# A hybrid attention and RWKV block on one core: the row factor on VectorE, low-rank weights split ahead, the second key norm inside the first half's recursion

## The chip, the cores and the metric

The kernel runs on one core of a Trainium2 chip. Its engines work side by side, each through its own queue of instructions in order: TensorE (PE) multiplies matrices into PSUM, VectorE (DVE), ScalarE (ACT) and GpSimd (POOL) work elementwise, and SyncE (SP) issues most of the transfers. The metric is device time in microseconds (us) of one execution; the time of a kernel is the median of several runs.

## What is computed

One layer over 256 tokens with a width of 2048, in fp32. Cut to what matters here:

```python
u = rms_norm(x)
proj = u @ w_in          # q, k, v of two attentions; r, k, v and low-rank inputs of RWKV-7; 3 branch gates
y_a = stick_breaking_attention(q_a, k_a, v_a)      # 4 heads of 128
y_b = forgetting_attention(q_b, k_b, v_b, log_f)   # 4 heads of 128

# RWKV-7: 16 heads of 64, chunks of 64 tokens
z = z + (z_prev - z) * mu
w_log = -softplus(-(w0 + tanh(wd) @ w_up)) - 0.5
a = sigmoid(a0 + ad @ a_up)
g = sigmoid(gd) @ g_up
kk = k * k_k
k = k * (1 + (a - 1) * k_a)
kk = kk / maximum(sqrt(sum(kk * kk)), 1e-12)       # the key norm, per head
state = state * w_t - (state @ kk_t) kka_t^T + v_t k_t^T;  y_t = state @ r_t
y_c = (group_norm(y) * ln_w + ln_b + bonus) * g    # the gate norm

m = g_a * (y_a @ w_a) + g_b * (y_b @ w_b) + g_c * (y_c @ w_c)
x = x + rms_norm(m @ w_out)
x = x + rms_norm(relu(rms_norm(x) @ w_up)**2 @ w_down)
```

## The kernel before

**Weights.** All weights are fp32 and stream from memory in halves of 128 x 1024 (512 KB), loaded on SP's queue (L145, three buffers `raw`). Each half is split into a high part `whi` on ACT (L152) and a low part `wlo` on DVE (L153), three buffers each; `wnext` keeps one half split ahead. A unit (`unit`, L178) multiplies two halves by the 16 packed parts `upk` of the normalized input: L168 for the high parts, L172 for the low ones, L176 for the last. Projections whose result is wanted with tokens on the partitions, and the branches, go through `tok` (L214, L198).

**The row factor.** The input is not normalized before the projections. The factor of each row, `rstd`, is made by `norm` (L375) from squares that `squares` sums on ACT and DVE, and is multiplied in behind each projection by `scaled` (L394), on POOL. The first eight units are the stick-breaking queries and keys (loop at L404), their output combined by `evac`. The projections of RWKV go through `shift` (L580): L585 on ACT, L586 on DVE, `scaled` at L587, L588 on ACT, L589 on DVE.

**What sets the order.** The order of PE's instructions is that of the code (L250). That of the other engines is set by a list scheduler. Beside the stream of weights run threads, Python generators: `tick` (L125) moves a clock by the estimated time of each pair of matmuls, and a thread goes on when its pause, the number that it last yielded, is over, or, where it yielded a name, some time after `mark` has set that name. The thread `mixers` (L959) runs the two attentions, the low-rank inputs (`rwkv_lora`, L596) and the RWKV in two halves of four head pairs each (`rwkv_half`, L627). `start` begins another thread; `finish` (L131) lets the clock run until no thread is left, here at L1062, before the third branch.

**A half of RWKV.** `rwkv_half` begins with the key norm: squares of the four keys (L655), split (L660, L661), summed per head by matmuls with `bones` (L668), then Ln and Exp on ACT (L672, L675) with a load of ACT's function table each (ACT_TABLE_LOAD), and a Newton step on DVE (L680 to L685). Then, for each pair, the low-rank up-projection L696 with the split weights `wl`; they are part of the tile `lows`. `lora_load` (L635) loads them on ACT's DMA queue and `lora_split` (L642) splits them: L645 on ACT, L647 twice on DVE. For the first pair the split stands behind the key norm (L689), for the others inside the pair before (L736). After the pairs comes a recursion of 31 steps on DVE (L792), then the loop over four chunks (L843): each chunk runs L847, the copies `rhs` (L851, L852), L860, the copies into `XT` (L864 on ACT, L865 on DVE, two of each), and L872, L876 and L881, which read `XT`. Behind the last chunk the thread `gate_norm` (L897) is started; the second half's key norm runs at the same time as the first half's gate norm. The second half waits for that before its chunks (L765).

**Around it.** Stick-breaking attention's sums are masked on POOL (L448, eight pieces), then split: L454 on ACT (`sbh`), L455 on DVE. The third branch (L1064 on) needs all of the gate norms' outputs `yc`.

Of the kernel before, what the change touches and what calls it, by code (L numbers as in the profile page):

```python
# [10 lines left out]
F32 = mybir.dt.float32  # L11
F32R = mybir.dt.float32r
# [38 lines left out]
def hybrid_block(ctx, tc, xt, x, gains, params, consts, lora, gup, wst, out):  # L51
# [13 lines left out]
    def nm(s):  # L65
        uid[0] += 1
        return f"{s}_{uid[0]}"
# [4 lines left out]
    def mps():  # L72
        return pm.tile([128, 512], F32, tag="mps", name=nm("mps"), bufs=4)
# [17 lines left out]
    def P(name, i=0, r=slice(0, 128)):  # L91
        return par[r, PC[name] + i:PC[name] + i + 1]
# [6 lines left out]
    def mark(key, value=True):  # L99
        done[key], at[key] = value, clock[0]  # L100
# [121 lines left out]
    def pin(ins):  # L222
        return tc.keep_in_program_order(ins)
# [168 lines left out]
        V.tensor_scalar(rt[:, :, 1], rt[:, :, 0], 0.5, None, ALU.mult)  # L392

    def scaled(d):  # L394
        G.tensor_tensor(d, d, rstd[0:d.shape[0]], ALU.mult)

    for i in range(2):
        wsplit(wraw())
# [5 lines left out]
    for h in range(8):  # L404
        ps = qb[h] if h < 3 else unit(upk)
        qk.append(g1())
        evac(ps, qk[h])
        if h == 3:
            ms = norm()
        if h == 5:  # L410
            turned_rstd(ms)
        for i in range(h + 1) if h == 3 else [h] if h > 3 else []:
            scaled(qk[i])
    done["sbq"], done["sbk"] = qk[:4], qk[4:]

# [208 lines left out]
        done["low"] = ((lows[:, 0], lows[:, 2]), (lows[:, 1], xal), lows[:, 3].rearrange("p (a b) -> p a b", a=2))  # L624
        yield 2.0

    def rwkv_half(hf):  # L627
        PR = range(4 * hf, 4 * hf + 4)
        xw, xa, wl = done["low"]
        kn, kx = {}, {}  # L630
        B6 = rp.tile([128, 6, T], F32, tag="b6", name=nm("b6"), bufs=1)
        rin = [B6[:, i, :] for i in range(4)]
        lor = {}

        def lora_load(p):  # L635
            if p in PR:
                lor[p] = rp.tile([128, 2, 128], F32, tag="zx", name=nm("lor"), bufs=1)
                for r in (0, 64):
                    nc.scalar.dma_start(out=lor[p][r:r + 64], in_=lora.rearrange("(s r) c -> r s c", s=2)
                                        [:, :, p * 128:p * 128 + 128])  # L640

        def lora_split(p):  # L642
            if p in PR:
                raw = lor[p]
                pin(A.activation(wl, raw, AF.Copy))  # L645
                for i, r in enumerate((slice(64, 128), slice(0, 64))):
                    V.tensor_tensor(wl[r, i], raw[r, i], wl[r, i].bitcast(F32), ALU.subtract)  # L647

        lora_load(PR[0])
        if hf:  # L650
            yield 8.0
        for i, p in enumerate(PR):
            yield f"k{p}"
            kx[p] = done[f"k{p}"]
            A.activation(rin[i], kx[p], AF.Square, scale=P("kk", p))  # L655
        sq, sqh = [], []
        for i2 in range(2):
            s = B6[:, 2 * i2:2 * i2 + 2, :]
            hl = [rp.tile([128, 2, T], F32R, tag="BK", name=nm("sqh"), bufs=8) for _ in range(2)]
            A.activation(hl[0], s, AF.Copy)  # L660
            V.tensor_tensor(hl[1], s, hl[0].bitcast(F32), ALU.subtract)  # L661
            sqh.append(hl)
        yield 3.8
        for i2 in range(2):
            ri = B6[:, 2 * i2:2 * i2 + 2, :]
            ps = mps()
            for n, part in enumerate(sqh[i2]):
                PE.matmul(ps.rearrange("p (a b) -> p a b", a=2), bones, part, start=n == 0, stop=n == 1)  # L668
            sq.append(rp.tile([128, 2, T], F32, tag="At", name=nm("sq"), bufs=2))
            V.tensor_scalar(sq[i2], ps.rearrange("p (a b) -> p a b", a=2), 1e-24, None, ALU.max)  # L670
# [7 lines left out]
        for i2 in range(2):  # L678
            ri = B6[:, 2 * i2:2 * i2 + 2, :]
            V.tensor_scalar(ri, ri, 1024.0, None, ALU.mult)  # L680
            V.tensor_tensor(sc, ri, ri, ALU.mult)
            yield 2.0
            V.tensor_tensor(sc, sc, sq[i2], ALU.mult)
            V.tensor_scalar(sc, sc, -0.5, 1.5, ALU.mult, ALU.add)
            V.tensor_tensor(ri, ri, sc, ALU.mult)  # L685
            yield 3.0
        SC = rp.tile([128, 32, 128], F32, tag="SC", name=nm("SC"), bufs=1)
# [155 lines left out]
        for c in range(4):  # L843
            if c:
                for i, p in enumerate(PR):
                    for h, hc in enumerate(HC):
                        PE.matmul(xy[h][HC[i % 2 ^ h], 64 * (i // 2):64 * (i // 2) + 64], Bt[p][hc, c, 0:64],  # L847
                                  PB[hc, i, hc], start=False, stop=i >= 2)
            rhs = rp.tile([64, 2, 2, 2, 64], F32, tag="rh", name=nm("rh"), bufs=1)
            for g, hg in enumerate(HC):  # L850
                A.activation(rhs[:, 0, g], xy[0][hg, 0:128].rearrange("p (a b) -> p a b", a=2), AF.Copy)  # L851
                V.tensor_copy(rhs[:, 1, g], xy[1][hg, 0:128].rearrange("p (a b) -> p a b", a=2))  # L852
            yield 2.0
            more = known(c + 1) if c < 3 else iter([None] * 9)
            if c < 3:
                first = next(more)
            ps = mps()
            for i in range(4):
                for h, hc in enumerate(HC):
                    PE.matmul(ps[hc, 64 * i:64 * i + 64], SC[0:64, i * 8 + h * 4 + c, 0:64],  # L860
                              rhs[:, h, i % 2 ^ h, i // 2], start=i == 0, stop=i == 3)
                    xy = next(more)
            for d in range(2):
                A.activation(XT[d][0:64, :, c, HC[0]], duo(ps, HC[0], d), AF.Copy)  # L864
                V.tensor_copy(XT[d][0:64, :, c, HC[1]], duo(ps, HC[1], d))  # L865
            yield 2.2
            ps = mps()
            psp, psy = ps[:, 0:256], ps[:, 256:512]
            if c < 3:
                for i, p in enumerate(PR):  # L870
                    for h, hc in enumerate(HC):
                        PE.matmul(psp[hc, 64 * i:64 * i + 64], Kt[p][:, c, hc], XT[i // 2][:, i % 2, c, hc],  # L872
                                  start=i == 0, stop=i == 3)
            for i, p in enumerate(PR):
                for h, hc in enumerate(HC):
                    PE.matmul(psy[hc, 64 * i:64 * i + 64], XT[i // 2][:, i % 2, c, hc], SC[:, i * 8 + h * 4 + c, 64:128],  # L876
                              start=i == 0, stop=c == 0 and i == 3)
            if c:
                for i, p in enumerate(PR):
                    for h, hc in enumerate(HC):  # L880
                        PE.matmul(psy[hc, 64 * i:64 * i + 64], PB[:, i, hc], Bt[p][:, c, 64:128], start=False,  # L881
                                  stop=i == 3)
            if c < 3:
                for h, hc in enumerate(HC):
                    s, e = PB[hc, :, hc], ecol[hc, :, c:c + 1].to_broadcast([64, 4, 64])
# [770 lines left out]
```

## Time and profile before

| | |
|---|---|
| median of 3 runs | 1519.44 us (1519.37 to 1525.15) |
| the profiled execution | 1523.08 us |
| its span, first to last instruction | 1521.3 us |
| mean granted TensorE clock | 0.990 |
| ACT, share of the span | 62% |
| L153, the low parts, on DVE | 501 of 1232 ns |
| L152, the high parts, on ACT | 501 of 1056 ns |
| weight halves through SP's queue | 499, 4.3 us from issue to landing |

A row of the timeline gives start, duration, engine, line, operation, the tile written, the tile read, shapes and count, and in brackets the idle time before it with what ended it. Names in it are those of tiles, without numbers. Consecutive instructions of one kind are one row. Durations overlap a little, since an instruction's end is drained while the next begins. The granted clock is TensorE's, as a share of full speed.

### The profile page before, as it was taken

How to read it: one execution, taken by the hardware profiler on the slowest of the kernel's cores; microseconds unless marked ns; L12 is line 12 of the kernel's file. 1: busy time of each engine (PE TensorE's matmuls, PEld its weight loads, DVE VectorE, ACT ScalarE, POOL GpSimd, SP SyncE). 2: the span in 40 equal slices, each digit the busy share in tenths (PEclk: the TensorE clock that was granted, in tenths of full speed). 3: DMA queues.
4: the chain of work that ended last, by engine and by line, in shares of the span. 5: the costliest groups of instructions: out<-in, count | busy, mean ns of one | idle time of the engine just before them, and what ended most of it. 6: DMA issues, size and time to landing. Idle time of an engine off the chain costs nothing.

```text
span 1521.3 us, 22774 instructions
## 1 busy us (share of the span) xinstructions
PE 1489.9 (98%) x8401; PEld 1253.3 (82%) x8401; DVE 1210.3 (80%) x1644; ACT 937.7 (62%) x1398; POOL 139.2 (9%) x203
## 2 busy tenths in 40 slices
PE   8999999999998999999999999999999999999997
PEld 7888887888777888778887888888888888888885
DVE  7566577779768789658655788989899999899986
ACT  7465666554557554565444676777677676676763
POOL 0232011320000100000000000000000000000000
PEclk9999999999999999999999999999999999999999
DMA  7545454444634545545695568788888888988874
GB/s 257 185 146 179 170 179 158 160 161 167 206 136 146 172 160 193 175 145 180 238 302 190 201 201 251 245 246 258 263 249 232 259 256 240 272 249 252 274 250 151
DMA packets 107616, 317.71 MB, mean 209 GB/s; under 512 B 10736, under 2 KB 14704, under 8 KB 107248
## 3 DMA queue, kind: packets, MB, share of 16 engines
q1 hardware_dynamic: 94832, 284.91, 54.4%
q0 software_dynamic: 8064, 29.36, 10.3%
q10 hardware_dynamic: 4608, 1.97, 0.5%
q8 instruction: 66, 1.08, 0.3%
q14 instruction: 46, 0.38, 0.1%
HBM read 282.65 MB, written 4.19 MB: 189 GB/s over the span
## 4 chain that ended last, share of the span: by engine, by line
PE 64%; DVE 2%; issue 1%; DMA 1%; ACT 1%; POOL 0%; POOLq 0%; DVEq 0%; ACTq 0%
PE gps L214 18%; PE gps L168 14%; PE gps L172 8%; PE gps L198 5%; PE mps L1386 3%; PE mps L1388 3%; PE mps L1387 3%; PE gps L1388 2%; PE gps L1386 2%; PE gps L1387 2%; PE gps L176 1%; DVE wlo L153 1%; DMA sp<-in_wst_dram 1%; PE mps L745 0%; ACT whi L152 0%
## 5 line engine op out<-in xcount | busy, mean ns | idle before, releaser
L153 DVE TENSOR_TENSOR wlo<-raw,whi 128x1024 fp32r<-128x1024 f32 x501 | 613.3, 1232 | 169.5 <-ACT whi L152 158.2
L152 ACT ACTIVATE whi<-raw 128x1024 fp32r<-128x1024 f32 x501 | 527.1, 1056 | 251.9 <-PE gps L214 113.1
L168 PE MATMUL gps<-pk,whi 128*128 128x512 f32 x1366 | 348.2, 394 | 2.2 <-ACT whi L152 2.1
L168 PEld LDWEIGHTS gps<-pk,whi 128*128 128x128 f32 x1366 | 254.2, 190 | 52.6 <-ACT whi L152 2.4
L214 PE MATMUL gps<-whi,pk 128*128 128x512 f32 x1144 | 288.9, 392 | 0.0
L214 PEld LDWEIGHTS gps<-whi,pk 128*128 128x128 f32 x1144 | 212.6, 188 | 44.3
L172 PEld LDWEIGHTS gps<-pk,wlo 128*128 128x128 f32 x1456 | 200.3, 192 | 14.4 <-DVE wlo L153 0.2
L172 PE MATMUL gps<-pk,wlo 128*128 128x256 f32 x1456 | 205.4, 284 | 0.0
L214 PE MATMUL gps<-wlo,pk 128*128 128x512 f32 x572 | 156.0, 392 | 0.3 <-DVE wlo L153 0.3
L214 PEld LDWEIGHTS gps<-wlo,pk 128*128 128x128 f32 x572 | 106.3, 188 | 23.2 <-DVE wlo L153 1.1
L1252 DVE TENSOR_TENSOR sp<-raw,sp 128x1024 fp32r<-128x1024 f32 x67 | 81.7, 1219 | 3.3 <-ACT sp L1251 3.1
L1278 ACT ACTIVATE sp<-gps 128x512 f32<-128x512 f32 x52 | 31.1, 598 | 82.9 <-PE gps L176 82.9
L1251 ACT ACTIVATE sp<-raw 128x1024 fp32r<-128x1024 f32 x67 | 70.6, 1053 | 13.6 <-PE mps L1387 4.7
L1348 POOL DMA_DIRECT2D raw<-raw x40 | 34.9, 873 | 426.2 <-DVE raw L1345 121.3
L198 PE MATMUL gps<-whi,pk 128*128 128x512 f32 x264 | 72.0, 394 | 0.0
L1386 PE MATMUL mps<-whi,fm 128*128 128x512 f32 x168 | 66.1, 394 | 0.0
L1388 PE MATMUL mps<-wlo,fm 128*128 128x512 f32 x168 | 65.7, 391 | 0.4 <-DVE wlo L153 0.2
L1387 PE MATMUL mps<-whi,fm 128*128 128x512 f32 x168 | 65.8, 392 | 0.0
L198 PEld LDWEIGHTS gps<-whi,pk 128*128 128x128 f32 x264 | 49.6, 190 | 10.5 <-ACT whi L152 0.2
L1388 PE MATMUL gps<-wlo,fm 128*128 128x512 f32 x126 | 49.2, 391 | 0.4 <-DVE wlo L153 0.4
L1386 PE MATMUL gps<-whi,fm 128*128 128x512 f32 x126 | 49.2, 391 | 0.0
L1345 DVE TENSOR_TENSOR raw<-raw,raw 128x1024 f32<-128x1024 f32 x40 | 48.8, 1220 | 0.4
(378 smaller groups left out, 1997.8 us busy)
## 6 DMA issues: line engine op xcount, KB each, us to landing
raw<-in_wst_dram SPq DMA_DIRECT2D x499, 512.0 KB, 4.3
raw<-raw POOLq DMA_DIRECT2D x40, 512.0 KB, 6.7
sp<-in_wst_dram SPq DMA_DIRECT2D x16, 512.0 KB, 5.8
raw<-sp POOLq DMA_DIRECT2D x8, 512.0 KB, 6.6
sp<-raw POOLq DMA_DIRECT2D x8, 512.0 KB, 8.5
x<-in_x_dram SPq DMA_DIRECT2D x8, 256.0 KB, 5.2
xs<-x SPq DMA_DIRECT2D x2, 1024.0 KB, 3.9
x<-xs SPq DMA_DIRECT2D x4, 512.0 KB, 6.0
```

Source lines behind the costliest of these rows:

```text
L152: A.activation(hi, raw, AF.Copy)
L153: V.tensor_tensor(lo, raw, hi.bitcast(F32), ALU.subtract)
L168: PE.matmul(ps, hi[:, i * 128:i * 128 + 128], pks[i], start=first and i == 0, stop=False)
L172: PE.matmul(ps[:, 0:T], lo[:, i * 128:i * 128 + 128], pks[i][:, 0:T], start=False, stop=False)
L198: PE.matmul(ps[tt], pks[k][:, c:c + 128], w[:, (k - k0) * 512:(k - k0) * 512 + 512], start=k == 0 and part == 0 and w is hl[0], stop=w is ...
L214: PE.matmul(ps[tt], pks[k][:, c:c + 128], w[:, (k - k0) * 512:(k - k0) * 512 + 512], start=k == 0 and part == 0 and w is hl[0], stop=False)
L1251: A.activation(hi, raw, AF.Copy)
L1252: V.tensor_tensor(lo, raw, hi.bitcast(F32), ALU.subtract)
L1345: V.tensor_tensor(x, x, z, ALU.add)
L1386: PE.matmul(Q[f], p, w, start=d == 0 and i == 0, stop=False)
L1387: PE.matmul(Q[f], pl, w, start=False, stop=False)
L1388: PE.matmul(Q[f], p, wl, start=False, stop=d == nd - 1 and i == 1)
```

## The change

- `scaled` multiplies on DVE (`V`) and not on POOL (`G`).
- `norm`, the turning of its result and the first scalings come one unit later in the loop over the first eight units.
- The key norm is a function of its own, `key_norm`. In the first half it runs where it ran. For the second half it is started as a thread within the first half's chunk loop, behind chunk 0; it takes the pairs of tiles one after the other there, and puts its split parts into the buffer `Ti` that the recursion has left.
- `lora_split` of a half's first pair comes ahead of the key norm, and the scheduler is no longer told to keep it in program order. In the second half it comes 4.0 after the start; the half then waits for the names "gate0" (the first pair of gate norm 0) and "kn1" (the key norm).
- The pauses in `gate_norm` are those of the second half for both halves; a step of the second half's recursion pauses 0.75 and not 0.5.

```diff
     def scaled(d):
-        G.tensor_tensor(d, d, rstd[0:d.shape[0]], ALU.mult)
+        V.tensor_tensor(d, d, rstd[0:d.shape[0]], ALU.mult)
...
-        if h == 3:
+        if h == 4:
             ms = norm()
-        if h == 5:
+        if h == 6:
             turned_rstd(ms)
-        for i in range(h + 1) if h == 3 else [h] if h > 3 else []:
+        for i in range(h + 1) if h == 4 else [h] if h > 4 else []:
             scaled(qk[i])
...
-    def rwkv_half(hf):
+    kin = {}
+
+    def key_norm(hf):
         PR = range(4 * hf, 4 * hf + 4)
...
-            A.activation(rin[i], kx[p], AF.Square, scale=P("kk", p))
-        sq, sqh = [], []
...
+            A.activation(rin[i], done[f"k{p}"], AF.Square, scale=P("kk", p))
+        sq = []
+        for both in ((0, 1),) if hf == 0 else ((0,), (1,)):
+            sqh = []
+            for i2 in both:
+                s = B6[:, 2 * i2:2 * i2 + 2, :]
+                if hf == 0:
+                    hl = [rp.tile([128, 2, T], F32R, tag="BK", name=nm("sqh"), bufs=8) for _ in range(2)]
+                else:
+                    t = rp.tile([128, 4, T], F32R, tag="Ti", name=nm("sqh"), bufs=1)
+                    hl = [t[:, 0:2], t[:, 2:4]]
+                A.activation(hl[0], s, AF.Copy)
+                V.tensor_tensor(hl[1], s, hl[0].bitcast(F32), ALU.subtract)
+                sqh.append(hl)
+            yield 3.8
+            for hl in sqh:
+                ps = mps()
+                for n, part in enumerate(hl):
+                    PE.matmul(ps.rearrange("p (a b) -> p a b", a=2), bones, part, start=n == 0, stop=n == 1)
+                sq.append(rp.tile([128, 2, T], F32, tag="At", name=nm("sq"), bufs=2))
+                V.tensor_scalar(sq[-1], ps.rearrange("p (a b) -> p a b", a=2), 1e-24, None, ALU.max)
+        if hf:
+            yield 2.0
         for i2 in range(2):
             A.activation(B6[:, 2 * i2:2 * i2 + 2, :], sq[i2], AF.Ln, scale=float(2.0 ** 20))
...
             V.tensor_tensor(ri, ri, sc, ALU.mult)
             yield 3.0
+        kin[hf] = rin
+        mark(f"kn{hf}")
+
+    def rwkv_half(hf):
...
+        kx = {p: done[f"k{p}"] for p in PR} if hf else {}
...
-                pin(A.activation(wl, raw, AF.Copy))
+                A.activation(wl, raw, AF.Copy)
...
+        lora_load(PR[0])
+        if hf:
+            yield 4.0
+            lora_split(PR[0])
+            yield "gate0"
+            yield "kn1"
+        else:
+            for p in PR:
+                yield f"k{p}"
+                kx[p] = done[f"k{p}"]
+            lora_split(PR[0])
+            yield from key_norm(0)
+        rin = kin[hf]
...
-        lora_split(PR[0])
...
-            yield 0.5 + n * m * 3.2e-3
+            yield (0.75 if hf else 0.5) + n * m * 3.2e-3
...
+            if c == 0 and hf == 0:
+                start(key_norm(1))
             if c < 3:
...
-        yield 5.0 if hf else 7.0
+        yield 5.0
...
-        yield 2.5 if hf else 4.5
+        yield 2.5
...
+            if i == 0:
+                mark(f"gate{hf}")
```

In the changed kernel the lines of the key norm are L635 (squares), L646 and L647 (split), L653 (matmuls), L655, L659 (Ln), L662 (Exp) and L667 to L672; those of `lora_split` are L693 and L695, the up-projection is L718, the chunk loop's copies are L873, L874, L886 and L887, and its matmuls L869, L882, L894, L898 and L903.

How it moves instructions is seen at three places. A row of the order gives the line, the operation, and the tiles written and read, with the program's numbers behind their names.

ACT, at the end of stick-breaking attention's sums (`sbh` is written by L454, `whi` are weights' high parts, L227 is `evac`). Before:

```order
L227 ACTIVATE tmp_898<-gps_849 128x256
L152 ACTIVATE whi_937<-raw_935 128x1024
L152 ACTIVATE whi_965<-raw_963 128x1024
L454 ACTIVATE sbh<-sbt 128x768 x2
L227 ACTIVATE tmp_958<-gps_902 128x256
L152 ACTIVATE whi_993<-raw_991 128x1024
```

With the change:

```order
L152 ACTIVATE whi_937<-raw_935 128x1024
L454 ACTIVATE sbh<-sbt 128x768
L152 ACTIVATE whi_965<-raw_963 128x1024
L454 ACTIVATE sbh<-sbt 128x768
L227 ACTIVATE tmp_958<-gps_902 128x256
L152 ACTIVATE whi_993<-raw_991 128x1024
```

The first of the two conversions moves ahead of a weight's high part; the second keeps its place ahead of the next.

DVE, at the low-rank weights of the first half's first pair (`lows` written by `lora_split`, `wlo` the weights' low parts, `b` the key norm's tile, `foxt` the forgetting attention's). Before:

```order
L153 TENSOR_TENSOR wlo_2502<-raw_2499,whi_2501 128x1024
L683 TENSOR_TENSOR b_399_2271<-b_399_2271,sq_2340 128x512
L586 TENSOR_TENSOR tmp_2490<-gps_2438,tmp_2489 128x256
L684 TENSOR_SCALAR b_399_2271<-b_399_2271 128x512
L685 TENSOR_TENSOR b_399_2271<-b_399_2271 128x512
L153 TENSOR_TENSOR wlo_2524<-raw_2521,whi_2523 128x1024
L589 SCALAR_TENSOR_TENSOR g_442_2488<-tmp_2490,omu,zp_2491 128x256
L647 TENSOR_TENSOR lows<-lor_2272,lows 64x128 x2
```

With the change:

```order
L153 TENSOR_TENSOR wlo_1720<-raw_1717,whi_1719 128x1024
L395 TENSOR_TENSOR tmp_1686<-tmp_1686,rstd_310 128x256
L153 TENSOR_TENSOR wlo_1753<-raw_1750,whi_1752 128x1024
L589 SCALAR_TENSOR_TENSOR g_285_1684<-tmp_1686,omu,zp_1687 128x256
L695 TENSOR_TENSOR lows<-lor_2271,lows 64x128 x2
L586 TENSOR_TENSOR tmp_1741<-gps_1694,tmp_1740 128x256
L395 TENSOR_TENSOR tmp_1741<-tmp_1741,rstd_310 128x256
L539 SCALAR_TENSOR_TENSOR foxt<-mps_1758,foxt 128x128
```

The split stood in row 247 of DVE's order and now stands in row 180, and L395 stands between DVE's other rows.

ACT, in chunk 1 of the first half's chunk loop (`rh` and `XT` are the chunk's copies, `sqh`, `sq` and `b` the second half's key norm). Before:

```order
L152 ACTIVATE whi_4211<-raw_4209 128x1024
L851 ACTIVATE rh_4192<-mps_4098 64x128 x2
L152 ACTIVATE whi_4285<-raw_4283 128x1024
L864 ACTIVATE XT_3445<-mps_4220 64x2x64
L864 ACTIVATE XT_3446<-mps_4220 64x2x64
L152 ACTIVATE whi_4316<-raw_4314 128x1024
```

With the change:

```order
L152 ACTIVATE whi_4227<-raw_4225 128x1024
L873 ACTIVATE rh_4200<-mps_4098 64x128 x2
L152 ACTIVATE whi_4301<-raw_4299 128x1024
L646 ACTIVATE sqh_4217<-b_773_4166 128x512
L659 ACT_TABLE_LOAD
L659 ACTIVATE b_773_4166<-sq_4215 128x512
L886 ACTIVATE XT_3445<-mps_4236 64x2x64
L662 ACT_TABLE_LOAD
L662 ACTIVATE b_773_4166<-b_773_4166 128x512
L886 ACTIVATE XT_3446<-mps_4236 64x2x64
L152 ACTIVATE whi_4337<-raw_4335 128x1024
```

Five rows of the key norm come to stand between the weight's high part and the second copy into `XT`.

More of the change, by code (lines that the diff above doesn't have):

```diff
@@ L625, in rwkv_lora @@
         yield 2.0
-    def rwkv_half(hf):
+    kin = {}
+    def key_norm(hf):
         PR = range(4 * hf, 4 * hf + 4)
-        xw, xa, wl = done["low"]
-        kn, kx = {}, {}
         B6 = rp.tile([128, 6, T], F32, tag="b6", name=nm("b6"), bufs=1)
         rin = [B6[:, i, :] for i in range(4)]
[L633 to L644, printed above, removed]
-                pin(A.activation(wl, raw, AF.Copy))
[L646 to L651, printed above, removed]
@@ L652, in rwkv_half @@
         for i, p in enumerate(PR):
             yield f"k{p}"
-            kx[p] = done[f"k{p}"]
-            A.activation(rin[i], kx[p], AF.Square, scale=P("kk", p))
-        sq, sqh = [], []
[L657 to L670, printed above, removed]
+            A.activation(rin[i], done[f"k{p}"], AF.Square, scale=P("kk", p))
@@ L686, in rwkv_half, with lora_load, lora_split @@
             yield 3.0
+        kin[hf] = rin
+        mark(f"kn{hf}")
+    def rwkv_half(hf):
+        PR = range(4 * hf, 4 * hf + 4)
+        xw, xa, wl = done["low"]
+        kn, lor = {}, {}
+        kx = {p: done[f"k{p}"] for p in PR} if hf else {}
+        def lora_load(p):
+            if p in PR:
+                lor[p] = rp.tile([128, 2, 128], F32, tag="zx", name=nm("lor"), bufs=1)
+                for r in (0, 64):
+                    nc.scalar.dma_start(out=lor[p][r:r + 64], in_=lora.rearrange("(s r) c -> r s c", s=2)
+                                        [:, :, p * 128:p * 128 + 128])
+        def lora_split(p):
+            if p in PR:
+                raw = lor[p]
+                A.activation(wl, raw, AF.Copy)
+                for i, r in enumerate((slice(64, 128), slice(0, 64))):
+                    V.tensor_tensor(wl[r, i], raw[r, i], wl[r, i].bitcast(F32), ALU.subtract)
+        lora_load(PR[0])
[11 more added lines that the diff above has]
+        rin = kin[hf]
         SC = rp.tile([128, 32, 128], F32, tag="SC", name=nm("SC"), bufs=1)
         At, Bt, Kt, bon = {}, {}, {}, {}
-        lora_split(PR[0])
         ecol = rp.tile([128, 4, 4], F32, tag="ecol", name=nm("ecol"), bufs=2)
```

## The prediction

> **What bounds the kernel now.** I read the page's engine shares first, then TensorE's waits, then its timeline and the granted clock around each long wait.
>
> ```profile
> PE 1489.9 (98%) x8401; PEld 1253.3 (82%) x8401; DVE 1210.3 (80%) x1644; ACT 937.7 (62%) x1398; POOL 139.2 (9%) x203
> PE mps L696 <- DVE lows L647: 6.3, 2, 3.3
> PE gps L198 <- DVE wlo L153: 2.3, 1, 2.3
> PE gps L168 <- ACT whi L152: 2.1, 1, 2.1
> PE mps L378 <- DVE a L373: 2.1, 1, 2.1
> ```
>
> TensorE (PE) is busy 98% of the span, and no matmul is added or removed. So only its idle time, and the time in which it works at a lower clock, can change. The wait list (total us, times, longest) names few places. These four rows are five waits; the two of 487 to 491 us lie together, so I speak of places 1 to 4 in order of time.
>
> ```profile
> 34.64 1.13 PE L378 MATMUL mps<-a,con 128*128 128x256 f32 x4 [2.06 <-DVE a L373]
> 107.69 3.00 PE L168 MATMUL gps<-pk,whi 128*128 128x512 f32 x8 [2.12 <-ACT whi L152]
> 108.00:109.00 1.00, 1.00 (x5) 0.81 0.00 0
> 109.00:110.00 1.00, 1.00 (x3) 0.50 0.28 37
> ...
> 111.00:112.00 1.00, 1.00 (x7) 0.50 0.80 250
> 263.38 0.98 PE L696 MATMUL mps<-lows 128*128 128x256 f32 x3 [3.33 <-DVE lows L647]
> 263.00:264.00 1.00, 0.62 (x3) 0.50 0.29 78
> ...
> 268.00:269.00 1.00, 1.00 (x4) 0.50 0.11 43
> 487.00 0.81 PE L198 MATMUL gps<-wlo,pk 128*128 128x512 f32 x2 [2.33 <-DVE wlo L153]
> 490.76 1.14 PE L696 MATMUL mps<-lows 128*128 128x256 f32 x3 [2.95 <-DVE lows L647]
> 491.00:492.00 1.00, 1.00 (x5) 0.50 0.90 352
> ...
> 493.00:494.00 1.00, 1.00 (x3) 0.50 0.31 91
> ```
>
> The bracket is the idle time before the row. In the rows with a colon the numbers are the window's length, PE's busy time, the granted clock and the DMA's share and rate. Places 2, 3 and 4 are followed by TensorE at half clock; between the first and the last row shown it stays at 0.50. A busy microsecond at clock c loses 1 − c. Place 2 loses 0.19 + 3 × 0.50 = 1.7 us this way, place 3 loses 0.62 × 0.5 + 5 × 0.5 = 2.8, place 4 loses 3 × 0.50 = 1.5. Place 1 loses nothing this way. Idle time and clock loss together: 2.1 + (2.1 + 1.7) + (3.3 + 2.8) + (2.3 + 3.0 + 1.5) = **18.8 us**. That is all that the change can win.
>
> **The change part by part.** *The norm, a unit later.* At place 1 L378 waits for the last sum of squares:
>
> ```profile
> 33.90 0.68 DVE L373 TENSOR_TENSOR a<-a 128x512 f32<-128x512 f32 x1
> 35.42 2.18 PE L168 MATMUL gps<-pk,whi 128*128 128x512 f32 x8
> 40.95 0.40 PE L176 MATMUL gps<-pk,whi 128*128 128x512 f32 x1
> ```
>
> The sum ends at 34.6. The unit that now stands ahead of L378 takes from 35.42 to 40.95 and a little, some 5.6 us; started where PE now falls idle (34.64 − 2.06 = 32.6), it ends at 38.2, well behind the sum. The 2.1 us go. Nothing needs the norm in that unit; the five scalings behind it come a unit later, and their readers (the attention's scores) not before the values' product.
>
> *The row factor on VectorE (L395).* All 43 multiplications leave POOL:
>
> ```profile
> L395 POOL TENSOR_TENSOR tmp<-tmp,rstd x27: 727/833/2320, 90.0 to 337.4; 128x256 f32<-128x256 f32 x26, 36x256 f32<-36x256 f32 x1
> L228 DVE TENSOR_TENSOR g<-gps,tmp x16: 410/418/426, 23.1 to 141.1; 128x256 f32<-128x256 f32 x16
> 259.51 0.42 DVE L586 TENSOR_TENSOR tmp<-gps,tmp 128x256 f32<-128x256 f32 x1
> 259.84 0.42 DVE L684 TENSOR_SCALAR b<-b 128x512 f32<-128x512 f32 x1
> ```
>
> L228 has the same engine, operation and shape, with 0.42 us, and small ones start 0.33 us apart. So DVE gets about 43 × 0.33 = 14 us more, spread over 43 to 340 us, where it has idle time. On the path that is nothing as long as no low part of a weight comes late. The bounds are 0 and one low part late by 0.33 us for every third of the 24 shifts, 2.6 us; I take 0.4, near the lower end, because no wait of PE for wlo stands in the wait list before 480 us.
>
> *Place 2.* ACT works in order, and the conversions of the stick-breaking sums (L454) stand ahead of the weight's high part that L168 waits for. The second L454 waits for POOL:
>
> ```profile
> 105.57 0.84 ACT L454 ACTIVATE sbh<-sbt 128x768 fp32r<-128x768 f32 x1 [2.30 <-POOL sbt L448]
> 102.36 0.74 POOL L395 TENSOR_TENSOR g<-g,rstd 128x256 f32<-128x256 f32 x1
> 103.06 2.48 POOL L448 TENSOR_TENSOR sbt<-sbt,con 128x128 f32<-128x128 f32 x4
> ```
>
> With L395 gone from POOL the second L454 comes 0.70 us earlier (103.06 − 102.36), and the wait is 2.12 − 0.70 = 1.4 us. The order also puts the first subtraction of L445 ahead of a weight's low part and of the second L444, so that POOL starts sooner; that I put at another 0.75. I take a remaining wait of **0.65 us** (bounds 0 and 2.1) without the loss of clock.
>
> *Place 3.* L696 waits for the low-rank weights' second part (L647), issued behind the key norm's last steps:
>
> ```profile
> 261.31 1.21 DVE L153 TENSOR_TENSOR wlo<-raw,whi 128x1024 fp32r<-128x1024 f32 x1
> 262.95 0.60 DVE L647 TENSOR_TENSOR lows<-lor,lows 64x128 fp32r<-64x128 f32 x2
> ```
>
> Its load (on ACT's DMA queue, which carries no weights) keeps its place at the head of the half, and the split now stands 67 rows earlier on DVE, among the forgetting attention's scores. No other operand of L718 (L696 before) is late: the lows themselves are made in the stage ahead. The weights that PE needs next are split in the order they were in. So 3.3 + 2.8 us go, or at worst one low part of 1.2 us and the clock stay, if another small step takes L647's place.
>
> *Place 4.* Here DVE did gate norm 0 and key norm 1 together, some 8 us of steps of the key norm (near 4 a pair, worked out below) between the weights. They leave, and the first split, which L696 waited for, is done in the chunk loop's time or before. What stays is a run of 15 small steps between two low parts (rows 554 and 570 of DVE's order now). At 0.33 us from start to start the second is there as PE asks; at their full 0.42 us it comes 1.75 us late. I take **0.3 us**.
>
> *The key norm in the chunk loop: what is new.* It brings table loads and six steps on ACT and DVE between the copies on which each chunk hangs. Rows of before for the chunk c = 1, and the norm's own steps where they stand now:
>
> ```profile
> 424.52 1.06 ACT L152 ACTIVATE whi<-raw 128x1024 fp32r<-128x1024 f32 x1 [1.06 <-issue]
> 427.20 0.27 ACT L864 ACTIVATE XT<-mps 64x128 f32<-64x128 f32 x1 [0.88 <-DVE XT L865]
> 427.50 0.29 DVE L865 COPY XT<-mps 64x128 f32<-64x128 f32 x1 [0.34 <-ACT XT L864]
> 428.39 0.69 PE L872 MATMUL mps<-XT,Kt 128*64 128x64 f32 x16
> 470.93 1.28 ACT L675 ACT_TABLE_LOAD   x1
> 472.22 0.63 ACT L675 ACTIVATE b<-b 128x512 f32<-128x512 f32 x1
> ```
>
> Before, the copies were done at 427.8, 0.6 us ahead of L872. Now ACT has, behind the weight's high part (425.6): a copy 0.63, a table load 1.28, Ln 0.63, the first XT copy 0.27, a table load 1.28, Exp 0.63, the second XT copy 0.27: 430.6, and DVE's copy 0.29: 430.9. PE wants that half of XT at 428.39, plus the norm's two matmuls and the first eight of L894, 0.8: 429.2. A new wait of **1.7 us**. For c = 2 DVE holds four of the norm's steps ahead of its last copy:
>
> ```profile
> 438.32 0.28 DVE L865 COPY XT<-mps 64x128 f32<-64x128 f32 x1
> 438.89 0.69 PE L872 MATMUL mps<-XT,Kt 128*64 128x64 f32 x16
> ```
>
> L667 and L671 at 0.42 (as L684), L668 and L670 at 0.68 (as L373, the same shape) make 2.2; the copy had 0.29 to spare and the first eight matmuls give 0.3: **1.6 us**. For c = 3, 0.3. Bounds: 0, if the norm's steps fall into the engines' idle time in each chunk, and 2.5 us in each of three chunks. Behind the waiting L894 on PE stand the chunk's other matmuls and then the next weights', all in the order written by hand, so each wait goes into the time whole.
>
> A table load here is followed by its function at once (470.93 + 1.28 = 472.21). The Trainium skill, "ScalarE: Activation LUTs", section "What ACT_TABLE_LOAD costs", adds a drain of about 1.38 us to each load, 2.66 us in all; by it the two loads of c = 1, and those of c = 2, would make each wait longer by 2.8. No drain is seen in these rows.
>
> *The clock.* Idle 2.06 us cost no clock at place 1, 2.12 cost 1.7 us at place 2. Two new waits of 1.6 and 1.7 lie just under both, in a stage with several pauses; I charge one loss, **1.7 us** (bounds 0 and three).
>
> The Trainium skill, "TensorE: Matmul & The Clock Gate", Part 1, halves the clock after a whole idle window of some 3.4 us, windows running free. By it the new waits would cost no clock, and the sum would lack the 1.7. Place 2 speaks against it as a strict bound: 2.12 us were enough.
>
> The sum: −18.8 + 0.4 + 0.65 + 0.3 + 1.7 + 1.6 + 0.3 + 1.7 = **−12.15 us**. The profiled execution took 1523.08 us (its span is 1521.3, with 1.8 around it), so it would be 1510.9. The median of the runs is 1519.44, 3.6 lower, and the difference carries over: **1507.3 us**.
>
> *The longer pauses in the second half's recursion* add 31 × 0.25 = 7.75 us to the order's clock. They issue nothing. Cover: the second half's first pair stands sooner in PE's order, and the last gate matmul, which stood 6 matmuls ahead of the third branch, now stands 18 ahead of it. I take 0; the bound is 7.75 us, if the tail of gate norm 1 is late by all of that.
>
> **The rivals.**
> (a) *The new waits leave the clock at full*: −13.85, 1505.6 us. Place 1 speaks for it, place 2 against.
> (b) *The key norm takes most of it back.* Three waits of 2.5 us, each with 1.7 of clock, are 12.6, and with 0.4 + 0.65 + 0.3 the net is −4.9: 1514.6 us. For it: the copies had 0.3 to 0.6 us to spare. Against it: ACT is busy 62% and fills in where it waits anyway.
> (c) *VectorE becomes the bound.* With the 14 us more, low parts come late behind L395: place 3 keeps 1.2 + 2.8, place 4 1.75 + 1.5; instead of the 0.3 these are 7.25, net −5.2: 1514.2 us. Against it: DVE's 80% is a mean, but the whole 18.8 us come from few places.
> (d) *Place 2 does not do what is said*: POOL is only 0.70 sooner, 1.4 us remain with 1.7 of clock: +2.45, 1509.8 us.
> (e) *Table loads at the longer price*: +5.6, 1512.9 us. The page on activation tables stands behind it, the row of 470.93 against it.
> (f) *Slower: the norm becomes one chain with the chunks.* ACT and DVE work in order, so once a chunk's copies stand behind steps that wait for each other, all of the norm stands on the path: per pair on ACT two loads and three steps, 2 × 1.28 + 3 × 0.63 = 4.45 us, on DVE 3 × 0.42 + 4 × 0.68 = 4.0, for two pairs 16.9, with three clock losses 22. With the upper bounds at places 2 and 4 (3.8 and 3.25) and 0.4 this is 29.4, net +10.6: 1530.0 us. Slower by 7.6 us it is from where four fifths of the norm's time are waited for; by my count it is 3.6 of 16.9.
>
> **How the numbers follow.** Forecast 0.40, (a) 0.15, (b) 0.17, (c) 0.10, (d) 0.08, (e) 0.03, (f) 0.07. A measurement of this kernel tells about 0.5% from no change, 7.6 us: 1511.8 to 1527.0. The forecast, (a) and (d) lie below, and of (b) and (c), which spread by some 3 us, a fifth: faster 0.68 (0.63 + 0.05). (f) is slower, 0.07. The rest is 0.25. The range goes from 1502.0, where of all that is added only 1.4 us of the two new waits are left (1519.44 − 18.8 + 1.4), to 1517.0, the upper end of (b); outside are (f) and some tails.
>
> **What the profile would show.** No wait of PE at L378, none at L718 (the old L696) near 260 or 485 us, a wait under 1 us at L168 near 105. POOL without L395, DVE with 43 of it at 0.42 us. In the chunk loop PE waiting at L894 or L898 for the XT copies L886/L887, 1 to 2.5 us twice, near 415 to 440 us, and the granted clock under 1.0 behind one of them. Wrong would be the prediction if DVE stands full between 185 and 345 us with PE waiting for wlo, if the later recursion in the second half (its pauses are longer) makes the last gate matmuls late for the third branch, or if a wait that I have not listed takes the old ones' place.

## The result, and the profile after

The changed kernel takes **1504.34 us** (median of 4 runs, 1502.33 to 1507.66) against 1520.65 us before (4 runs): a ratio of 0.989, with a 95% interval from 0.9862 to 0.9918. The forecast was 1507.3, range 1502.0 to 1517.0. The profiled executions took 1523.08 and 1504.03 us, with spans of 1521.3 and 1502.3.

The page of the changed kernel, its engine line, and TensorE's waits, the rows of 0.3 us or more that belong to the stages of the change (us in total, times, longest):

```profile
PE 1482.0 (99%) x8401; PEld 1249.1 (83%) x8401; DVE 1215.5 (81%) x1687; ACT 938.5 (62%) x1398; POOL 91.3 (6%) x160
PE mps L894 <- DVE XT L887: 1.6, 3, 1.0
PE mps L894 <- ACT XT L886: 1.2, 1, 1.2
PE gps L168 <- ACT whi L152: 0.4, 1, 0.4
PE mps L898 <- DVE XT L887: 0.3, 1, 0.3
```

All rows of before have gone but L168's, which fell from 2.1 to 0.4. New are the waits in the chunk loop, 3.1 us together, for the copies into `XT`, where the prediction put them. DVE took over 43 rows from POOL, and its busy time rose by 5 us only.

As a yardstick for the stages that the change touches I use the second group of transposes behind the middle norm, which all kernels here run. Its row in the timeline of TensorE, before and with the change (start, duration, idle time before it in brackets):

```profile
835.17 1.90 PE L1162 MATMUL mps<-ident,x 128*128 128x128 f32 x8 [1.87 <-DVE x L1130]
```

```profile
817.11 1.81 PE L1188 MATMUL mps<-ident,x 128*128 128x128 f32 x8 [1.87 <-DVE x L1156]
```

It starts 18.06 us earlier. The stages behind it are the same in both kernels; from this row to the end of the span it is 685.2 to 688.9 us in the twelve profiles, so I leave them out below. Each row of a timeline is one execution's: in a second profile of the changed kernel (e10 below) the yardstick row starts 1.15 us later than in the first, and the profiled execution of before, 1523.08 us, lies above the median of 1520.65.

Where the 18.06 us come from is seen by setting the same matmul of both timelines side by side:

| the matmul | start before | start after | earlier by |
|---|---|---|---|
| first of the stick-breaking values, behind place 1 | 58.69 | 56.52 | 2.17 |
| high parts of the unit's second half, behind place 2 | 112.14 | 106.85 | 5.29 |
| first of a unit at 293 us, behind place 3 | 293.56 | 282.11 | 11.45 |
| in the recursion's stage, ahead of the chunk loop | 404.54 | 390.61 | 13.93 |
| behind the chunk loop | 453.94 | 445.08 | 8.86 |
| transposes behind the middle norm | 835.17 | 817.11 | 18.06 |

Places 1 to 3 gave 2.2, 3.1 and 6.2 us; the forecast had 2.1, 3.2 and 6.1. Two steps are not as forecast. Between 293 and 404 us, where the forecast had nothing, 2.5 us went. In the chunk loop 5.1 us are lost. The four matmuls of L653, which came there from the second half, take 0.47 us a pair, 0.9 together; they come back as a gain behind the loop, where place 4 goes. The rest is the two chunks with new waits: from the first row of L872 (now L894) to the next weight's matmul, chunk 1 took 1.55 us and takes 3.45, chunk 2 took 1.55 and takes 3.72. That is 4.1 us, of which 2.8 are idle time; the interrupted matmuls overlap less with each other (L894's rows add up to 3.3 us of busy time, L872's to 2.1).

The chunk c = 1 in ACT's timeline with the change, the rows of the prediction's count:

```profile
411.56 0.61 ACT L646 ACTIVATE sqh<-b 128x512 fp32r<-128x512 f32 x1
412.19 1.28 ACT L659 ACT_TABLE_LOAD   x1
413.48 0.63 ACT L659 ACTIVATE b<-sq 128x512 f32<-128x512 f32 x1
414.14 0.27 ACT L886 ACTIVATE XT<-mps 64x128 f32<-64x128 f32 x1
414.43 1.28 ACT L662 ACT_TABLE_LOAD   x1
415.72 0.63 ACT L662 ACTIVATE b<-b 128x512 f32<-128x512 f32 x1
416.26 0.25 ACT L886 ACTIVATE XT<-mps 64x128 f32<-64x128 f32 x1
```

```profile
416.56 0.33 PE L894 MATMUL mps<-XT,Kt 128*64 128x64 f32 x2 [1.18 <-ACT XT L886]
417.07 0.39 PE L894 MATMUL mps<-XT,Kt 128*64 128x64 f32 x5 [0.17 <-DVE XT L887]
428.57 0.63 PE L894 MATMUL mps<-XT,Kt 128*64 128x64 f32 x8 [0.40 <-DVE XT L887]
430.25 0.39 PE L894 MATMUL mps<-XT,Kt 128*64 128x64 f32 x5 [1.05 <-DVE XT L887]
```

The second fence is TensorE's: 1.18 + 0.17 = 1.35 us in chunk 1 (forecast 1.7) and 0.40 + 1.05 = 1.45 us in chunk 2 (forecast 1.6). ACT's steps stand back to back; no time of its own follows a table load. The granted clock in the microseconds behind these waits is 1.00 in this execution:

```profile
429.00:430.00 1.00, 0.20 (x3) 1.00 0.06 16
430.00:431.00 1.00, 0.75 (x25) 1.00 0.04 4
431.00:432.00 1.00, 1.00 (x22) 1.00 0.93 270
```

### The profile page after: what moved, and what is told of

It reads as the page before. It is cut to its first block, busy times and chain, and to the rows that moved or that the text cites. A ratio compares the mean times of both kernels' runs of the same rounds, so it can differ in the third digit from the quotient of the medians.

```text
span 1502.3 us, 22802 instructions
## 1 busy us (share of the span) xinstructions
PE 1482.0 (99%) x8401; PEld 1249.1 (83%) x8401; DVE 1215.5 (81%) x1687; ACT 938.5 (62%) x1398; POOL 91.3 (6%) x160
## 4 chain that ended last, share of the span: by engine, by line
PE 69%; DVE 1%; issue 1%; POOL 0%; POOLq 0%; ACT 0%; DVEq 0%; ACTq 0%
PE gps L214 20%; PE gps L168 15%; PE gps L172 8%; PE gps L198 5%; PE mps L1412 3%; PE mps L1413 3%; PE mps L1414 3%; PE gps L1414 3%; PE gps L1412 2%; PE gps L1413 2%; PE gps L176 1%; PE mps L767 0%; PE mps L976 0%; DVE wlo L153 0%; PE mps L1103 0%
## 5 line engine op out<-in xcount | busy, mean ns | idle before, releaser
L153 DVE TENSOR_TENSOR wlo<-raw,whi 128x1024 fp32r<-128x1024 f32 x501 | 608.3, 1223 | 162.7 <-ACT whi L152 147.8
L168 PE MATMUL gps<-pk,whi 128*128 128x512 f32 x1366 | 346.4, 393 | 0.6 <-ACT whi L152 0.4
L168 PEld LDWEIGHTS gps<-pk,whi 128*128 128x128 f32 x1366 | 253.0, 189 | 50.5 <-ACT whi L152 0.6
```

The source lines that it names most:

```text
L153: V.tensor_tensor(lo, raw, hi.bitcast(F32), ALU.subtract)
L168: PE.matmul(ps, hi[:, i * 128:i * 128 + 128], pks[i], start=first and i == 0, stop=False)
```

## The experiments

Each kernel is told apart by its waits and by the yardstick row; of a single run, a difference in that row of about 1 us isn't told from chance, since two executions of the changed kernel are 1.15 us apart. Times of one run are given as such; the kernel before took 1520.6 to 1522.4 us (medians) beside them.

**e1: the freed split alone.** The kernel before with one word less:

```diff
-                pin(A.activation(wl, raw, AF.Copy))
+                A.activation(wl, raw, AF.Copy)
```

> The kernel before with one edit: lora_split's ACT conversion is no longer kept in program order; where it stands in the code, the norm, the row factor on POOL and the key norm stay as before. Theory A (the freed order alone does it): the split moves far ahead on DVE, the waits of L696 near 260 us (3.3, and 2.8 of clock) and near 490 us (2.95, and most of the 1.5 of clock) go, 8 to 10.5 us in all; L378's 2.1, L168's 2.1 and L198's 2.3 stay. Theory B (the place in the code, ahead of the key norm, does it): the waits of L696 stay and the time is that of before within 2 us.

1516.94 us (10 runs) against 1522.37, ratio 0.9965 (0.9951 to 0.9979). TensorE's longest waits between 100 and 700 us:

```profile
PE gps L198 <- DVE wlo L153: 2.3, 1, 2.3
PE gps L168 <- ACT whi L152: 2.1, 1, 2.1
PE mps L771 <- DVE SC L755: 0.6, 1, 0.6
```

L696 is gone, at 260 and at 490 us, though the split stands behind the key norm in the code as before. The yardstick row starts at 827.22, 7.95 us earlier than before, just under theory A's 8 to 10.5; the medians differ by 5.4 us. So theory A holds in kind: what holds the split back is that its conversion is kept in program order. The scheduler moves it far ahead as soon as it may, and the new place in the code, which is the visible part of this edit, isn't needed for it. Whether the new place would do it with the conversion still kept in order wasn't run. It also parts place 4 into two causes: the 2.95 us for the lows go here, the 2.3 us for a low part stay.

**e2: the row factor back on POOL**, the rest as changed:

```diff
-        V.tensor_tensor(d, d, rstd[0:d.shape[0]], ALU.mult)
+        G.tensor_tensor(d, d, rstd[0:d.shape[0]], ALU.mult)
```

> The changed kernel with the row factor back on POOL. Theory A (POOL's row ahead of the second group of masks caused place 2): L168's wait near 105 us is 1.4 to 2.1 again, with up to 1.7 of clock behind it, 1 to 3.4 us longer than the changed kernel. Rival (the later norm and the other order on DVE cured it): the wait stays under 0.5 and the time is within 0.5 us. VectorE as a bound would show the other way: small waits for wlo between 185 and 345 us that go now; I expect none.

One run of 1512.32 us. TensorE's waits between 100 and 400 us:

```profile
PE gps L168 <- ACT whi L152: 2.1, 1, 2.1
PE mps L793 <- DVE SC L777: 0.6, 1, 0.6
PE mps L571 <- ACT foxt L566: 0.4, 1, 0.4
PE gps L214 <- DVE wlo L153: 0.4, 1, 0.4
PE mps L767 <- DVE At L745: 0.3, 1, 0.3
```

L168's wait is back, and the clock falls behind it. But there is more, which neither theory had: other waits of 0.3 to 0.6 us come (the changed kernel has only L168's 0.4 in this stretch), and the yardstick row starts at 824.26, 7.15 us later than in the changed kernel. Their cause is seen around 317 us, on POOL and on ACT:

```profile
316.18 1.65 POOL L395 TENSOR_TENSOR tmp<-tmp,rstd 128x256 f32<-128x256 f32 x1 [3.47 <-DVE tmp L586]
317.86 0.51 ACT L588 ACTIVATE zp<-tmp,par 128x256 f32<-128x256 f32 x1 [3.18 <-POOL tmp L395]
```

ACT stands 3.18 us idle for one factor, with a weight's high part behind it. Of that time POOL's multiplication is 1.65 us; before it, POOL itself waits for DVE's L586.

**e3: the norm back at its place**:

```diff
-        if h == 4:
+        if h == 3:
...
-        if h == 6:
+        if h == 5:
```

(with the scalings' bounds back as well)

> The changed kernel with the norm back behind unit 3 and the turning behind unit 5. Theory A: L378 waits 2.1 us again for the sum of squares near 33 us and the first 50 us take 2.1 more; nothing else moves. It also asks the clock again: after 2.06 idle the clock stayed at 1.00 before. If the length of the wait decides, it stays at 1.00 here; if the moment decides, it may be 0.50 for some us, 1.7 more.

One run of 1509.0 us; the row that answers to place 1:

```profile
33.48 1.13 PE L378 MATMUL mps<-a,con 128*128 128x256 f32 x4 [1.68 <-DVE a L373]
```

The wait is back with 1.7 us, and the clock stays at 1.00; as the wait is shorter than the 2.06 us of before, this doesn't part its length from its moment. From 32 to 58 us this execution loses 1.9 us on the changed one, of which 0.9 us make up for a start that was that much sooner. The yardstick row, 818.50, is 1.4 us later; a further small wait (L1103, 0.4 us) comes ahead of it.

**e4: the second key norm back in the second half**, both pairs together, beside gate norm 0:

```diff
-            if c == 0 and hf == 0:
-                start(key_norm(1))
...
-            yield "gate0"
-            yield "kn1"
+            yield 4.0
+            yield from key_norm(1)
```

> The changed kernel with the second key norm back at the head of the second half, beside gate norm 0, both pairs together as before; the freed split stays ahead. Theory A (two separate causes at place 4): the chunk loop's waits for XT (2.8 us with c = 1 and 2) go, L718 does not wait, but DVE is full between 450 and 480 us and L198 or L214 waits 2 to 3 us for a wlo, with 0 to 1.7 of clock: within 2.5 us of the changed kernel either way. Rival (the chunk loop is the better place by far): 5 us or more longer than the changed kernel.

One run of 1510.07 us; the yardstick row starts at 822.81, 5.7 us later than in the changed kernel. TensorE's waits from 395 to 720 us:

```profile
PE gps L214 <- DVE wlo L153: 2.1, 1, 2.1
PE mps L972 <- DVE gup L933: 1.9, 1, 1.9
PE mps L972 <- DVE gup L934: 0.5, 2, 0.3
```

The chunk loop's waits go, as both said. The wait for a low part between 450 and 480 us comes back, as theory A said. But a third one comes that neither had: the last gate matmuls (L972, 681 us) wait for their weights' split behind gate norm 1. So the rival's number is met (5.7), by a cause that it didn't name: the second half gets late as a whole. That the key norm inside the first half cures this as well is what this run shows; how much of it the longer pauses add isn't parted here.

**e5: the row factor on VectorE alone**, in the kernel before (the edit of e2 the other way round).

> The kernel before with one edit: the row factor on VectorE. Theory A (it wins more than place 2: POOL's late factors also held ACT, and with it VectorE's small steps and the pairs' copies): L168's 2.1 us and its 1.7 of clock near 107 us go (about 3), and the small waits of PE between 240 and 370 us (L771, the low parts before the recursion) go as well, 2 to 3.5 us more: 5 to 6.5 us in all. Theory B (my forecast's term: it only clears place 2, and costs 0 to 2.6 elsewhere): 1 to 3.2 us. The waits of L696 and of L378 stay in both.

1516.27 us (8 runs) against 1521.45, ratio 0.9959 (0.9946 to 0.9973). Waits of TensorE between 100 and 700 us:

```profile
PE mps L696 <- DVE lows L647: 5.1, 2, 3.0
PE gps L198 <- DVE wlo L153: 2.3, 1, 2.3
PE gps L168 <- ACT whi L152: 0.4, 1, 0.4
```

Up to the first high parts of the third unit behind place 2's (start 127.96 before, 123.51 here, with 1.3 of it from the first 60 us) 3.15 us go; between 293 and 404 us another 2.7. The small waits of L771 and of the low parts there have gone. Theory A holds for both stretches, the forecast's term for L395 doesn't. A third gain was in no expectation: place 3 gets 3.8 us shorter, since L696 now waits 2.10 us and the clock doesn't fall. So the yardstick row (825.24) is 9.9 us earlier than before, more than the 5 to 6.5 expected, while the medians differ by 5.2:

```profile
257.70 0.61 PE L696 MATMUL mps<-lows 128*128 128x256 f32 x3 [2.10 <-DVE lows L647]
```

**e6: the pause of 0.5 in the second recursion again.**

> The changed kernel with the second half's recursion pausing 0.5 again. I took these pauses at 0 us: within 0.5 us of the changed kernel up to the middle norm, with no new wait. Rival (the pause gives VectorE time, so that the second half's steps are not waited for): waits of PE of 1 us or more between 560 and 680 us for the transposes or the triangular products, 1 to 4 us.

One run of 1506.8 us; the yardstick row starts at 817.74, 0.63 later, and L894's waits for `XT` are 4 and not 3 (1.9 us and not 1.6). That is less than the 1.15 us between two executions of the changed kernel, so neither a gain nor a cost of these pauses is seen, and the forecast's 0 us stands. The shorter pauses in `gate_norm`, which are part of the change too, weren't tried alone.

**e7: one pair of table loads for both pairs of tiles.** Ln and Exp of the key norm are kept in program order:

```diff
-            A.activation(B6[:, 2 * i2:2 * i2 + 2, :], sq[i2], AF.Ln, scale=float(2.0 ** 20))
+            pin(A.activation(B6[:, 2 * i2:2 * i2 + 2, :], sq[i2], AF.Ln, scale=float(2.0 ** 20)))
...
-            A.activation(ri, ri, AF.Exp, scale=-0.5)
+            pin(A.activation(ri, ri, AF.Exp, scale=-0.5))
```

> The changed kernel with Ln and Exp of the key norm kept in program order, so that the two pairs of the second key norm share one pair of table loads, between chunks 1 and 2. Theory A (the table loads and the norm's steps between the copies are the wait): the wait for XT in chunk 1 (1.35 us) goes, in chunk 2 the copies rh and the next high part come later by up to 1.5 us: 0 to 2 us shorter than the changed kernel. Rival (any place in the loop costs the same): 2.5 to 3 us of waits in chunk 2.

**e8: the same, both loads behind chunk 2's copies** (the pause ahead of Ln 4.0 and not 2.0).

> As e7, with the pause ahead of the two Ln at 4.0 and not 2.0, so that both table loads come behind the copies into XT of chunk 2. Theory A: no wait for XT in chunks 1 and 2; VectorE's first norm step waits for Exp and holds the state's update of chunk 2 by 1 to 2 us: 1 to 2.5 us shorter than the changed kernel. Rival: the held update and the later high part cost as much as the copies did, no gain.

**e9: e7, and the Newton steps kept in order too**:

```diff
-            V.tensor_scalar(ri, ri, 1024.0, None, ALU.mult)
+            pin(V.tensor_scalar(ri, ri, 1024.0, None, ALU.mult))
```

> As e7, and the first step of each Newton iteration (L667) kept in program order too, so that VectorE does the norm's steps behind the state's update of chunk 2 and not ahead of its copies. Theory A: no wait for XT in chunk 1, at most 0.4 us in chunk 2, 0.3 in chunk 3: 2 to 2.8 us shorter than the changed kernel up to the middle norm. Rival (the steps only move the wait to chunk 3 or to the second half, which waits for the key norm): under 1 us.

**e10: the changed kernel once more**, beside e9.

> The changed kernel once more on the same chip, to stand beside e9: by its own trace the waits of the chunk loop are 2.8 us with c = 1 and 2 and the clock stays at 1.00 there. If the clock's fall hangs on the moment and not on these waits' length, this run may show 0.50 behind one of them; I expect 1.00. Against e9, theory A gives 0.1 to 0.2% more time here, under what the rounds can settle; the rival none.

The waits of TensorE in the chunk loop, of e7 and then of e9:

```profile
PE mps L894 <- DVE XT L887: 1.7, 2, 1.0
PE mps L898 <- DVE XT L887: 0.3, 1, 0.3
```

```profile
PE mps L894 <- DVE XT L887: 1.0, 1, 1.0
PE mps L898 <- DVE XT L887: 0.3, 1, 0.3
```

| kernel | us | yardstick row starts |
|---|---|---|
| e7 | 1505.12 (one run) | 815.94 |
| e8 | 1505.67 (one run) | 817.74 |
| e9 | 1502.57 (4 runs), ratio 0.9874 (0.9851 to 0.9897) | 815.25 |
| e10 | 1505.39 (4 runs), ratio 0.9889 (0.9867 to 0.991) | 818.26 |

With fewer table loads, and the norm's steps behind the copies, the wait for `ACT XT L886` goes, and of 3.1 us 2.0 are left in e7 and 1.3 in e9. In chunk 2 the norm's steps were the wait: it falls from 1.45 us to 0.71 in e7, where two of the four table loads are saved, and to nothing in e9. In chunk 1 they were so only in part: both expected no wait there, and 0.97 of 1.35 us stay in both, since a weight's high part on ACT and its low part on DVE now stand between the two copies. So theory A of e7 and e9 holds about for the time and for chunk 2, and fails for chunk 1. In e8 the rival was right: PE waits for `XT` for 1.0 and 1.1 us and 0.3 for the held update of the state, and nothing is won. By the yardstick e9 is 1.9 us ahead of the first profile of the changed kernel and 3.0 ahead of the second. Its median is 2.8 us lower in the same session, but the intervals overlap; it beats the kernel before, and against the changed one the runs don't settle it.

The clock in e10, windows behind the second wait of the chunk loop, is where the expectation failed:

```profile
429.00:430.00 1.00, 0.68 (x19) 0.88 0.06 16
430.00:431.00 1.00, 1.00 (x23) 0.50 0.87 209
431.00:432.00 1.00, 1.00 (x8) 0.50 0.80 315
432.00:433.00 1.00, 1.00 (x4) 0.50 0.00 0
433.00:434.00 1.00, 1.00 (x5) 0.91 0.00 0
```

The waits are the same two as in the first profile (1.18 and 1.05 us), and here the clock falls to 0.50 behind the second.

## Why the prediction was right, and where its sizes were off

**What the change removes** (18.8 us of idle time and clock loss at four places): right for places 1 to 3, each within 0.1 us by the table of starts. At place 4 the clock loss was put at 1.5 us from the windows 491 to 494; three more of the same view belong to it:

```profile
487.00:488.00 1.00, 0.81 (x2) 0.75 0.07 8
490.00:491.00 1.00, 0.24 (x1) 0.50 0.63 168
494.00:495.00 1.00, 1.00 (x5) 0.84 0.82 222
```

They add 0.20 + 0.12 + 0.16, so place 4 lost 2.0 us of clock. That TensorE's few long waits, and the time at half clock behind them, were all that could be won, was nearly right: it left out the 1.1 us of small waits between 325 and 355 us, and weight loads that came late there.

**L395 on VectorE**: the term that was mis-sized. The forecast put it at +0.4 us, because DVE gets more work. Measured, it is −2.5 us between 293 and 404 us in the changed kernel, −2.7 in e5, +2.9 when undone in e2 (from 3.35 us behind the changed kernel at 291 us to 6.2 at 339). The prediction priced the edit by the engine that takes the work and not by the engines that had waited for the one that loses it. ACT's row for this was in the trace before:

```profile
ACT zp L588 <- POOL tmp L395: 27.3, 24, 3.6
```

With ACT in order, 27.3 us of its waits stood ahead of high parts and of the pairs' copies. With the change it is 3.3 us:

```profile
ACT zp L588 <- DVE tmp L395: 3.3, 6, 1.3
```

And DVE didn't get 14 us busier: the groups of L153 between 42 us and the recursion, before and with the change, read

```profile
L153 DVE TENSOR_TENSOR wlo<-raw,whi 128x1024 fp32r<-128x1024 f32 x94 | 120.5, 1287 | 42.7 <-ACT whi L152 42.2
```

```profile
L153 DVE TENSOR_TENSOR wlo<-raw,whi 128x1024 fp32r<-128x1024 f32 x93 | 113.3, 1225 | 36.1 <-ACT whi L152 32.4 <-ACT foxt L566 1.2 <-ACT foxt L533 1.1
```

A low part took 1287 ns on average while POOL multiplied beside it, and 1225 ns without: some 6 us less for 93 of them. The edits alone say the same: with the row factor back on POOL (e2) the mean is 1293 ns in this stretch, with it on DVE in the kernel before (e5) 1224. The Trainium skill, "GPSIMD Engine Reference", section "Specifications", says that GpSimd's interfaces to SBUF are shared with VectorE, with contention for instructions with two SBUF inputs. L153 is one, and these rows agree.

**Place 2**: the step that was named is right: POOL's eight masks come together (one row of 7.43 us) and end at 100.8 us, and not at 105.5. The size is right by luck. The high part whose rest was forecast at 0.65 us isn't waited for at all; the 0.39 us measured are a new wait, for the high part before it, which now stands behind the first conversion:

```profile
99.14 0.85 ACT L454 ACTIVATE sbh<-sbt 128x768 fp32r<-128x768 f32 x1 [3.83 <-POOL sbt L448]
100.99 1.88 PE L168 MATMUL gps<-pk,whi 128*128 128x512 f32 x7 [0.39 <-ACT whi L152]
```

**Place 3**: the size was right, 6.1 us forecast and 6.2 measured, and so was its ground, that the split comes sooner on DVE. Which of the two edits brings it there the prediction didn't say: by e1 the freed order is enough.

**Place 4**: forecast a rest of 0.3 us, measured none; the run of 15 small steps on DVE took 5.8 us (468.28 to 474.08), 0.39 from start to start, between the 0.33 and the 0.42 that were counted, and no wait follows. Behind the chunk loop 18.06 − 8.86 = 9.2 us are won, 0.9 of them the matmuls of L653; the other 8.3 stand against a forecast of 6.8 − 0.3 = 6.5. Of the 1.8 us between them 0.3 is this rest and 0.5 the clock windows above; 1.0 isn't traced.

**The key norm in the chunk loop**: forecast 1.7 + 1.6 + 0.3, measured 1.35 + 1.45 + 0.29 as idle time, and 1.9 + 2.2 + 0 as time lost (the 0.29 stood there before). The counted chain on ACT was right step by step; the table loads took 1.28 us each, with no drain behind them, so the rival at 2.66 us falls.

**The clock**: charged 1.7 us, measured 0 in the first profile of the changed kernel and 0.68 × 0.12 + 3 × 0.50 + 0.09 = 1.7 us in e10, by the windows above. Both are executions of one kernel, so a charge with a chance was the right form; what decides between the two isn't shown here.

**The sum**: −12.15 against −16.3 by the medians and −18.06 by the yardstick. The difference of 5.9 us from the yardstick is L395 (2.9), the clock (1.7) and place 4 (1.8), less 0.5 in the chunk loop (4.1 us lost and not 3.6). That the median lands 3.0 us from the forecast owes something to chance too: the medians moved 1.8 us less than the yardstick row.

Of the rivals, (a) came true in the first profile, and half of the missing gain was outside of all of them: apart from (a), none was on the side of a larger gain. Rival (c), VectorE as the bound, is refuted: no wait of TensorE for a low part stands between 150 and 480 us.

## What to carry to other kernels

When work moves from one engine to another, look first at who waits for the engine that loses it: in-order engines pass a small late result on to everything behind it. Where a scheduler may reorder, look for the instruction that it may not move; here one such mark cost 5 us by the medians and 8 by the yardstick, and with it gone the code's order didn't have to change. A wait of about two microseconds on TensorE cost its length here, and in some places some 1.7 us of clock more.

## What the runs showed of the hardware

The half clock doesn't follow from the length of a wait alone. An idle time of 1.87 us ahead of the yardstick row was followed by a clock of 0.50 in all twelve profiles; 2.06 us at place 1 and 2.10 us in e5 (place 3) were not; 2.12 us at place 2 was; and 1.05 us, shortly behind 0.39, was in e10 and was not in the other profile of the same kernel. Behind waits of 1.05 and 2.1 us (e10, place 2) the loss was 1.7 us each, three whole windows at 0.50 and a little on both sides (e10's windows above), so the half clock lasted about 3.4 us. At place 3, and at place 4 in the kernel before and in e5, it lasted about 6.8 us, twice that (by the windows from 262.2 to 269.0 and from 487.5 to 494.3 us); there TensorE was idle for more than 1 us within the first half of it, and place 3 lost 2.8 us, e5's place 4 2.7. The Trainium skill, "TensorE: Matmul & The Clock Gate", Part 1, has a window of that length (3.4 us) that runs free of the program, which fits the length and the dependence on the moment. Its condition of a whole idle window isn't borne out: no idle time named here is as long as 3.4 us, and several were followed by half the clock.
